# A four-layer decoder trunk: where the transposes of the next sub-layer's tokens stand, and which engine fills four zero tiles

## The chip, the cores and the metric

The kernel runs on one core of a Trainium2 chip. The metric is the device time of one execution in microseconds (us), taken as the median of several runs. The engines are TensorE (PE in the profile, with its weight loads as PEld), VectorE (DVE), ScalarE (ACT), GpSimd (POOL) and SyncE (SP, which here only issues DMAs). Each engine takes its instructions strictly in the order in which the built program holds them.

## The reference

256 tokens of 1024 float32 numbers pass through eight sub-layers: stick-breaking attention, an MLP, a short gated convolution, an MLP, gated linear attention (GLA), an MLP, stick-breaking attention, an MLP. Each sub-layer is wrapped in two RMS norms, and every MLP is the same:

```
def squared_relu_mlp(xn, w_up, w_down):
    return jnp.square(jax.nn.relu(xn @ w_up)) @ w_down

for i in range(DEPTH):                       # DEPTH = 4
    xn = rms_norm(h, norm_gains[i, 0])
    m = ...                                  # mixer i % 3 on xn
    h = h + rms_norm(m, norm_gains[i, 1])
    f = squared_relu_mlp(rms_norm(h, norm_gains[i, 2]), ffn_w_up[i], ffn_w_down[i])
    h = h + rms_norm(f, norm_gains[i, 3])
```

## The kernel before

The 256 tokens are two tiles, t = 0 and t = 1, of 128 tokens each; the residual stream `h` stays in SBUF. Every float32 operand of a large product is split in two parts, hi (rounded) and lo (the rest), and a product is three matmuls: hi by hi, hi by lo, lo by hi. The weights stream in as units of 1024 columns (SP issues the DMA into a ring of 5 `raw` buffers, ACT makes `hi` at L202 and DVE makes `lo` at L203, in rings of 9, each unit in two halves); 6 units are asked for ahead of their use.

A sub-layer ends with a product whose result has tokens on partitions: `out_proj_steps` (L368) for the three mixers, `down` in `ffn` (L421) for the MLP. It does t = 0 first and then t = 1, and the last part of each tile is 8 k-steps of six matmuls of 512 columns (hi, lo, and hi again, two PSUM banks each). After the last k-step of a tile `finish` (L849) runs: `add_norm` (L240: the square sums on ACT at L237, the product with the gain on DVE at L250, the reciprocal root on POOL at L229 and L232, the new h on DVE at L253), then `pre_norm` (L264) for the next sub-layer (again a square sum on ACT, the gain at L271, the root on POOL, and the scaling of both halves of the row at L279 on DVE). Then `turned` (L282) puts eight 128x128 transposes on PE (L262), four into each of two `wk` tiles in PSUM, and `spread` (L288) writes them into the stationary operands `xth` (ACT, L222) and `xtl` (DVE, L223).

The next sub-layer begins with a product that needs all of `xth` and `xtl` of one token tile at a time: `x_proj_steps` (L323) in the mixers, `up_x` (L386) in the MLP, 8 k-steps of six matmuls for t = 0 and then 8 for t = 1. In `up_x` the result goes through ACT (relu, L398) and DVE (square, L400) and is itself transposed, 8 more instructions of L262.

The order on each engine is made by a scheduler: an instruction has a priority from its place in the text, `tc.high_priority(offset=...)` moves it ahead by an offset, and the scheduler fills each engine in the order of priority as it reckons operands to be ready. Before, the transposes of t = 0 have the offset 400 and those of t = 1 the offset -80 (`TP`, L855); `add_norm`, `pre_norm` and `spread` have 400 (`HP`). Stick-breaking attention also needs four tiles of 1024 columns filled with zeros (`qpad`), filled on POOL at L456 in both layers that use it.

In the names below `s` is a working tile, `acc` and `wk` are PSUM tiles, `cf` holds the identity matrix, `sm` the small results of a norm.

Of the kernel before, what the change touches and what calls it, by code (L numbers as in the profile page):

```python
# [9 lines left out]
F32 = mybir.dt.float32  # L10
F32R = mybir.dt.float32r
# [5 lines left out]
P = 128  # L17
# [3 lines left out]
SEQ = 256  # L21
# [40 lines left out]
def hybrid_kernel(ctx: ExitStack, tc: tile.TileContext, x, norm_gains, sb_w_qkv, sb_w_o,  # L62
                  conv_w_in, conv_w, conv_w_out, gla_w_in, gla_w_gate_up, gla_b_gate,
                  gla_head_norm, gla_w_o, ffn_w_up, ffn_w_down, const_f, const_i, out,
                  phases=None, LA=6, RAW=5, RING=9, SLOTS=20, HP=400, AP=200, EP=200, XP=-40, TP=(400, -80),
                  F1=5.9, F2=1.3, G0=2.0, G1=2.0, LAG=1, PS=2,
# [48 lines left out]

    # residual stream and constants
    h = []
# [17 lines left out]

    # ---- weights, in the order of their first use
    plan = []
    index = {}

    def add(key, w, k0, n, c0, b):  # L140
        """n k-tiles of b columns, in pieces of 1024 columns a partition."""
        a = UNIT // b
        for j in range(n // a):
            index[(key, j)] = len(plan)
            plan.append(((key, j), rows(w, k0 + j * a, a, c0, b), b))
# [73 lines left out]

    # ---- pieces  # L220
    def split(hi, lo, src):
# [18 lines left out]
    def add_norm(accs, l, i, t, dst=None):  # L240
        """h += norm(the columns in accs); stored in halves where dst is given."""
        g = gain(l, i)
        ag = scratch()
        ss = []
        c = 0
        for a in accs:
            cs = slice(c, c + a.shape[1])
            c += a.shape[1]
            ss.append(sumsq(a))
            nc.vector.tensor_tensor(out=ag[:, cs], in0=a, in1=g[:, cs], op=ALU.mult)  # L250
        r = rstd_of(ss[0], 1, *ss[1:])
        for n, cs in enumerate([slice(0, D)] if dst is None else [slice(0, 512), slice(512, D)]):
            nc.vector.scalar_tensor_tensor(out=h[t][:, cs], in0=ag[:, cs], scalar=r, in1=h[t][:, cs], op0=ALU.mult, op1=ALU.add)  # L253
            if dst is not None:
                (nc.sync, nc.scalar)[n].dma_start(out=dst[:, cs], in_=h[t][:, cs])
# [32 lines left out]
    def spread(ws, t):  # L288
        for half, w in enumerate(ws):
            wv = w.rearrange("p (a b) -> p a b", b=P)  # L290
            sl = (slice(None), slice(4 * half, 4 * half + 4), slice(t * P, (t + 1) * P))
            split(xth[sl], xtl[sl], wv)

    def banks(acc):
        return [acc[:, 0:512], acc[:, 512:1024]]

    def x_stat(acc, lh, ll, units, first, last):
        """acc[n] += x.T @ units; lh/ll(kt) stationary, units: list over kt of [(hi, lo) per n]."""
        for _ in x_stat_steps(acc, lh, ll, units, first, last):
            pass  # L300
# [17 lines left out]
    def wide(key, j):  # L318
        """a k-tile of 1024 columns as the moving side."""
        hi, lo = need(key, j)  # L320
        return [(hi[:, 0, n * 512:(n + 1) * 512], lo[:, 0, n * 512:(n + 1) * 512]) for n in range(2)]

    def x_proj_steps(acc, t, key):  # L323
        lh, ll = xs(t)
        for j in range(KT):
            yield from x_stat_steps(banks(acc), lh[j:], ll[j:], [wide(key, j)], j == 0, j == KT - 1)

# [6 lines left out]
    def w_stat_steps(o, key):  # L334
        """o [P, 2, 256] = (two 128-column blocks of the unit).T @ x.T"""
        for k in range(KT):
            hi, lo = need(key, k // 4)
            for j in range(2):
                cs = slice(j * P, (j + 1) * P)
                oj = o[:, j * SEQ:(j + 1) * SEQ]  # L340
                mm(oj, hi[:, k % 4, cs], xth[:, k, :], k == 0 and j == 0, False)
                mm(oj, hi[:, k % 4, cs], xtl[:, k, :], False, False)
                mm(oj, lo[:, k % 4, cs], xth[:, k, :], False, k == KT - 1)
            yield 0.65
# [5 lines left out]
    class Fill:  # L350
        """Steps of matmuls, emitted in between the steps of a chain."""

# [15 lines left out]
    def out_proj_steps(l, us, finish):  # L368
        for t in range(NT):
            acc = acc_tile()  # L370
            ts = slice(t * P, (t + 1) * P)
            for j in range(KT):
                yield from x_stat_steps(banks(acc), [us[j // 4][0][:, j % 4, ts]], [us[j // 4][1][:, j % 4, ts]],
                                        [wide((l, "o"), j)], j == 0, j == KT - 1)
            finish([acc], t)
# [3 lines left out]

    # ---- FFN  # L380
    def ffn(l, finish, final=False):
# [4 lines left out]
        def up_x():  # L386
# [3 lines left out]
            for t in range(NT):  # L390
                acc = acc_tile()
                lh, ll = xs(t)
                for k in range(4):
                    un = [need((l, "up", g, k)) for g in range(XG)]
                    ws = [[(hi[:, a, :], lo[:, a, :]) for hi, lo in un] for a in range(2)]
                    x_stat(banks(acc), lh[2 * k:], ll[2 * k:], ws, k == 0, k == 3)
                r = scratch()
# [23 lines left out]
        def down(g, ts_):  # L421
            for k in range(4):
                for t in ts_:
                    if accs[t] is None:
# [25 lines left out]

    # ---- stick-breaking attention
    def sb(l, finish):
        qpad = []
        for i in range(4):
            q = slot((P, 2, 2, SEQ), F32R)
            nc.gpsimd.memset(q.bitcast(F32), 0.0)  # L456
            qpad.append(q)
        vs = []
        if l == 0:
            # both token tiles are there from the start: they share each piece of the weights  # L460
            accs = [acc_tile() for _ in range(NT)]
            gens = [x_proj_steps(accs[t], t, (l, "v")) for t in range(NT)]
            for j in range(KT + LAG):
                for t in range(NT):
                    if 0 <= j - LAG * t < KT:
                        next(gens[t])
        for t in range(NT):
# [4 lines left out]
            else:  # L472
                nc.scalar.copy(out=v, in_=acc)
            vs.append(v)
        us = [u_pair(), u_pair()]

        def qk_steps(g, res):
            w = wk_tile()
            yield from w_stat_steps(w, (l, "q", g))
            # the queries of each head of a pair, padded with zeros in the other head's rows  # L480
            qs = []
# [86 lines left out]

    # ---- short gated convolution
    def conv(l, finish):  # L570
# [45 lines left out]

    # ---- gated linear attention
    def gla(l, finish):
# [25 lines left out]

        # the gates' logarithms, tokens on partitions
        w = wk_tile()
# [34 lines left out]
        def decays(t, pr):  # L681
            """exp of the summed log gates between each token and the middle of its block, two levels."""
            acc = acc_tile()
# [32 lines left out]
        def weigh(t, pr):  # L716
            """the decays times the keys (lower halves) and the queries (upper halves), in place."""
            ts = slice(t * P, (t + 1) * P)
# [101 lines left out]

    # ---- the trunk
    pre = {"ffn": 2}
# [23 lines left out]
    for n, (kind, l) in enumerate(phases):  # L846
        nxt = phases[n + 1] if n + 1 < len(phases) else None

        def finish(acc, t, kind=kind, l=l, nxt=nxt):  # L849
# [4 lines left out]
            if nxt:  # L854
                with tc.high_priority(offset=TP[t]):  # L855
                    ws = turned(xn, t)
                with tc.high_priority(offset=HP):
                    spread(ws, t)

# [31 lines left out]
```

## Time and profile before

| | |
|---|---|
| time, median of 3 runs | 1228.62 us (1225.62 to 1228.74) |
| profiled execution, first to last instruction (its span, the only time of its own that the profile gives) | 1226.1 us |
| PE matmuls busy | 1193.8 us, 97% of the span, 7260 instructions |
| DVE / ACT / POOL busy | 769.4 / 671.5 / 57.3 us |
| chain that ended last, by engine | PE 46%, DVE 1%, POOL 1%, ACT 1% |
| granted TensorE clock, mean | 0.996 |
| HBM | 213 MB read, 175 GB/s over the span |

PE is busy nearly all the time, so what can be read for a change of order is where PE is idle and what ended each idle stretch. In a timeline row the numbers are the start, the length, the engine, the line, the operation, output and inputs, how many instructions the row merges, and in brackets the idle time of that engine before it with what ended it. Matmuls are pipelined: a matmul's row is longer than the distance to the next one, so distances are taken between starts.

### The profile page before, as it was taken

The page shows a single profiled execution, that of the slowest core. Times are in us where ns is not written, and L with a number is a line of the kernel's source. Part 1 is how long each engine was busy: PE and PEld are TensorE (multiplying, and loading weights), DVE is VectorE, ACT ScalarE, POOL GpSimd, SP SyncE. Part 2 cuts the span into 40 slices and gives each one's busy share as a digit, 9 for nine tenths or more (in the row PEclk, how much of TensorE's full clock was granted, in tenths as well). Part 3 has the DMA queues.
Part 4 walks back from the last instruction along what each step waited for, and adds up shares of the span by engine and source line. Part 5 has one row for each costly group of instructions (what it writes and reads, how often), then busy time and mean ns, then how long its engine had stood idle before and what let it go on. Part 6 is the DMA issues. An engine that isn't in the chain of part 4 may idle for free.

```text
span 1226.1 us, 18808 instructions
## 1 busy us (share of the span) xinstructions
PE 1193.8 (97%) x7260; PEld 1052.0 (86%) x7260; DVE 769.4 (63%) x1199; ACT 671.5 (55%) x1192; POOL 57.3 (5%) x94
## 2 busy tenths in 40 slices
PE   5999999999999999999999999999999999999997
PEld 4988789988799789988789878999877987899986
DVE  6675775654777666555656677655556666765552
ACT  5677564543555465554563655645544876554551
POOL 2000100000100100000200120000011000000000
PEclk9999999999999999999999999999999999999999
DMA  7743467566476556666553345666646442666540
GB/s 246 261 135 106 138 192 223 187 190 205 138 223 191 164 182 221 189 189 214 166 195 127 114 143 189 210 194 188 204 154 202 122 149 95 203 205 191 189 154 35
DMA packets 123083, 215.28 MB, mean 176 GB/s; under 512 B 7729, under 2 KB 85681, under 8 KB 122994
## 3 DMA queue, kind: packets, MB, share of 16 engines
q1 hardware_dynamic: 122434, 213.28, 55.2%
q8 instruction: 57, 0.93, 0.3%
q10 hardware_dynamic: 432, 0.59, 0.1%
q0 software_dynamic: 128, 0.21, 0.1%
q14 instruction: 32, 0.26, 0.1%
HBM read 213.01 MB, written 1.05 MB: 175 GB/s over the span
## 4 chain that ended last, share of the span: by engine, by line
PE 46%; DVE 1%; issue 1%; POOL 1%; ACT 1%; DMA 0%; DVEq 0%; POOLq 0%
PE acc L112 26%; PE wk L112 18%; PE wk L262 1%; DVE lo L203 0%; POOL sm L229 0%; POOL sm L232 0%; DMA raw<-in_sb_w_qkv_dram 0%; DVE s L279 0%; ACT s L237 0%; POOL s L760 0%; ACT s L535 0%; ACT s L773 0%; ACT hi L202 0%; DVE s L759 0%; DVE s L775 0%
## 5 line engine op out<-in xcount | busy, mean ns | idle before, releaser
L203 DVE TENSOR_TENSOR lo<-raw,hi 128x512 fp32r<-128x512 f32 x768 | 501.0, 688 | 268.0 <-ACT hi L202 265.5
L202 ACT CAST hi<-raw 128x512 fp32r<-128x512 f32 x768 | 442.4, 618 | 346.9 <-PE wk L112 169.2
L112 PE MATMUL acc<-hi,s 128*128 128x512 f32 x1280 | 355.1, 391 | 0.0
L112 PE MATMUL wk<-xth,hi 128*128 128x256 f32 x1216 | 342.1, 281 | 0.4 <-DVE s L585 0.4
L112 PE MATMUL wk<-xtl,hi 128*128 128x256 f32 x1216 | 342.0, 281 | 0.0
L112 PE MATMUL wk<-xth,lo 128*128 128x256 f32 x1216 | 341.3, 281 | 0.0
L112 PEld LDWEIGHTS acc<-hi,s 128*128 128x128 f32 x1280 | 237.9, 188 | 49.2 <-ACT s L222 1.3
L112 PEld LDWEIGHTS wk<-xth,hi 128*128 128x128 f32 x1216 | 229.3, 189 | 2.6 <-issue 0.7
L112 PEld LDWEIGHTS wk<-xtl,hi 128*128 128x128 f32 x1216 | 229.1, 188 | 1.3 <-issue 0.2
L112 PEld LDWEIGHTS wk<-xth,lo 128*128 128x128 f32 x1216 | 229.5, 189 | 0.2 <-issue 0.2
L112 PE MATMUL acc<-lo,s 128*128 128x512 f32 x640 | 199.6, 390 | 0.0
L112 PEld LDWEIGHTS acc<-lo,s 128*128 128x128 f32 x640 | 120.0, 188 | 25.0
L112 PE MATMUL acc<-hi,xth 128*128 128x512 f32 x288 | 95.7, 409 | 1.1 <-ACT xth L222 1.1
L112 PE MATMUL acc<-hi,xtl 128*128 128x512 f32 x288 | 94.4, 406 | 0.0
L112 PE MATMUL acc<-lo,xth 128*128 128x512 f32 x288 | 93.6, 405 | 0.0
L112 PEld LDWEIGHTS acc<-hi,xth 128*128 128x128 f32 x288 | 54.7, 192 | 13.9 <-ACT xth L222 1.7
L229 POOL TENSOR_SCALAR sm<-sm 128x1 f32<-128x1 f32 (+1 forms) x32 | 17.1, 536 | 1058.1 <-ACT s L237 1050.8
L112 PEld LDWEIGHTS acc<-hi,xtl 128*128 128x128 f32 x288 | 54.8, 191 | 13.6
L112 PEld LDWEIGHTS acc<-lo,xth 128*128 128x128 f32 x288 | 54.7, 191 | 13.2 <-issue 0.2
L250 DVE TENSOR_TENSOR s<-acc,s 128x1024 f32<-128x1024 f32 (+1 forms) x17 | 19.7, 1160 | 65.0 <-ACT s L237 65.0
L262 PE MATMUL wk<-cf,s 128*128 128x128 f32 x224 | 38.3, 288 | 22.5 <-DVE s L279 11.5
L262 PEld LDWEIGHTS wk<-cf,s 128*128 128x128 f32 x224 | 26.9, 146 | 31.5 <-issue 15.5
(101 smaller groups left out, 776.5 us busy)
## 6 DMA issues: line engine op xcount, KB each, us to landing
raw<-in_ffn_w_up_dram SPq DMA_DIRECT2D x128, 512.0 KB, 3.8
raw<-in_ffn_w_down_dram SPq DMA_DIRECT2D x128, 512.0 KB, 3.6
raw<-in_sb_w_qkv_dram SPq DMA_DIRECT2D x48, 512.0 KB, 4.8
raw<-in_conv_w_in_dram SPq DMA_DIRECT2D x24, 512.0 KB, 3.8
raw<-in_gla_w_in_dram SPq DMA_DIRECT2D x24, 512.0 KB, 4.1
s<-in_norm_gains_dram SPq DMA_DIRECT2D x16, 512.0 KB, 5.1
raw<-in_sb_w_o_dram SPq DMA_DIRECT2D x16, 512.0 KB, 3.6
raw<-in_conv_w_out_dram SPq DMA_DIRECT2D x8, 512.0 KB, 3.5
```

What stands on the lines that cost most here:

```text
L112: nc.tensor.matmul(out=o, lhsT=l, rhs=r, start=start, stop=stop, skip_group_check=True)
L202: nc.scalar.copy(out=hi[:, cs], in_=raw[:, cs])
L203: nc.vector.tensor_tensor(out=lo[:, cs], in0=raw[:, cs], in1=hi[:, cs].bitcast(F32), op=ALU.subtract)
L229: nc.gpsimd.tensor_scalar(out=v, in0=ss, scalar1=EPS, scalar2=None, op0=ALU.add)
L250: nc.vector.tensor_tensor(out=ag[:, cs], in0=a, in1=g[:, cs], op=ALU.mult)
L262: nc.tensor.transpose(out=dst[:, j * P:(j + 1) * P], in_=src[:, j * P:(j + 1) * P], identity=ident)
```

## The change

Priorities no longer place the transposes. `finish` only puts the scaled tile in a list, `pending`, and the products call `turn_pending` at a fixed k-step: the products that end a sub-layer after their sixth k-step of t = 1 (`TURN[0]`; this turns the tokens of t = 0), and the products that begin one after their seventh k-step of t = 0 (`TURN[1]`; this turns the tokens of t = 1). The writes into `xth` and `xtl` keep their priority. In the second stick-breaking layer the four zero tiles are filled by DVE, after the values of t = 0 are copied, in place of POOL at the start of the layer; the first such layer is as before. The diff, without comment lines and with the loops that it goes through:

```
-                  ... XP=-40, TP=(400, -80),
+                  ... XP=-40, TURN=(6, 7),
...
+    pending = []
+
+    def turn_pending():
+        while pending:
+            xn, t = pending.pop()
+            ws = turned(xn, t)
+            with tc.high_priority(offset=HP):
+                spread(ws, t)
...
     def x_proj_steps(acc, t, key):
         for j in range(KT):
+            if j == TURN[1]:
+                turn_pending()
...
     def out_proj_steps(l, us, finish):
             for j in range(KT):
+                if j == TURN[0]:
+                    turn_pending()
...
         def up_x():
-                    x_stat(banks(acc), lh[2 * k:], ll[2 * k:], ws, k == 0, k == 3)
+                    for j, _ in enumerate(x_stat_steps(banks(acc), lh[2 * k:], ll[2 * k:], ws, k == 0, k == 3)):
+                        if 2 * k + j + 1 == TURN[1]:
+                            turn_pending()
...
         def down(g, ts_):
             for k in range(4):
+                if 4 * (g - 6) + k == TURN[0]:
+                    turn_pending()
...
     def sb(l, finish):
+        def padded(eng):
+            for i in range(4):
+                q = slot((P, 2, 2, SEQ), F32R)
+                eng.memset(q.bitcast(F32), 0.0)
+                qpad.append(q)
         qpad = []
-        for i in range(4):
-            q = slot((P, 2, 2, SEQ), F32R)
-            nc.gpsimd.memset(q.bitcast(F32), 0.0)
-            qpad.append(q)
+        if l == 0:
+            padded(nc.gpsimd)
...
             vs.append(v)
+            if l and t == 0:
+                padded(nc.vector)
...
         def finish(acc, t, kind=kind, l=l, nxt=nxt):
             if nxt:
-                with tc.high_priority(offset=TP[t]):
-                    ws = turned(xn, t)
-                with tc.high_priority(offset=HP):
-                    spread(ws, t)
+                pending.append((xn, t))
```

First place: PE at the end of the first attention layer, in the product of t = 1 (a k-step's matmuls are named by their weight, here `hi_1104` for the sixth and `hi_1184` for the seventh). Before:

```order
L112 MATMUL acc_1361<-hi_1050,s_378 128x512 x2
L112 MATMUL acc_1361<-hi_1104,s_377 128x512
L262 MATMUL wk_1347<-cf_84,s_1336 128x128 x4
L262 MATMUL wk_1348<-cf_84,s_1336 128x128 x4
L112 MATMUL acc_1361<-hi_1104,s_377 128x512
L112 MATMUL acc_1361<-lo_1105,s_377 128x512 x2
```

and now:

```order
L112 MATMUL acc_1347<-hi_1050,s_378 128x512 x2
L112 MATMUL acc_1347<-hi_1104,s_377 128x512 x2
L112 MATMUL acc_1347<-lo_1105,s_377 128x512 x2
L112 MATMUL acc_1347<-hi_1104,s_378 128x512 x2
L262 MATMUL wk_1384<-cf_84,s_1336 128x128 x4
L262 MATMUL wk_1385<-cf_84,s_1336 128x128 x4
L112 MATMUL acc_1347<-hi_1184,s_377 128x512 x2
```

The eight transposes of t = 0 stand five matmuls later, behind 36 of the 48 in place of 31; all seven sub-layer ends have this shift. On ACT at the same place (`hi` are weight casts, `xth` the write that the transposes release), before:

```order
L202 CAST hi_1296<-raw_1294 128x512 x2
L202 CAST hi_1310<-raw_1308 128x512
L222 CAST xth_93<-wk_1347 128x4x128
L222 CAST xth_93<-wk_1348 128x4x128
L202 CAST hi_1310<-raw_1308 128x512
```

and now:

```order
L202 CAST hi_1310<-raw_1308 128x512 x2
L202 CAST hi_1438<-raw_1436 128x512
L222 CAST xth_93<-wk_1384 128x4x128
L222 CAST xth_93<-wk_1385 128x4x128
L202 CAST hi_1438<-raw_1436 128x512
```

Two weight casts that stood behind the writes into `xth` stand ahead of them; DVE has the same with two `lo` ahead of `xtl`.

Second place: PE in the MLP that follows, in the product of t = 0 (`acc_1449`, now `acc_1435`). Before:

```order
L112 MATMUL acc_1449<-lo_1453,xth_93 128x512
L112 MATMUL acc_1449<-lo_1461,xth_93 128x512
L262 MATMUL wk_1431<-cf_84,s_1420 128x128
L112 MATMUL acc_1449<-hi_1452,xtl_94 128x512
L262 MATMUL wk_1431<-cf_84,s_1420 128x128
L112 MATMUL acc_1449<-hi_1460,xtl_94 128x512
L262 MATMUL wk_1431<-cf_84,s_1420 128x128
```

and now:

```order
L112 MATMUL acc_1435<-lo_1447,xth_93 128x512
L112 MATMUL acc_1435<-hi_1438,xtl_94 128x512
L112 MATMUL acc_1435<-hi_1446,xtl_94 128x512
L262 MATMUL wk_1542<-cf_84,s_1420 128x128 x4
L262 MATMUL wk_1543<-cf_84,s_1420 128x128 x4
L112 MATMUL acc_1435<-hi_1438,xth_93 128x512
```

The transposes of t = 1 stand together behind 42 matmuls; before they stood one by one between matmuls, the first behind 40. The first transposes behind matmuls stood at 42 in the convolution, 38 in GLA and 41 in the second attention layer, and stand at 42 in all of them now. The MLP's own transposes, of its squared result, stand behind 11 matmuls of t = 1 in place of 12.

Third place: the second attention layer. POOL before (`sm` are the steps of the norms of t = 1):

```order
L232 TENSOR_TENSOR sm_8949<-sm_8950,mhalf_91 128x1
L456 MEMSET s_8979 128x1024
L229 TENSOR_SCALAR sm_8960<-sm_8955 128x1
L456 MEMSET s_8981 128x1024
L232 TENSOR_TENSOR sm_8959<-sm_8960,mhalf_91 128x1
L456 MEMSET s_8983 128x1024
L456 MEMSET s_8985 128x1024
```

and DVE there now:

```order
L271 TENSOR_TENSOR s_8954<-h_81,s_8869 128x1024
L203 TENSOR_TENSOR lo_8997<-raw_8994,hi_8996 128x512
L279 TENSOR_SCALAR s_8954<-s_8954,sm_8959 128x512 x2
L203 TENSOR_TENSOR lo_8997<-raw_8994,hi_8996 128x512
L223 TENSOR_TENSOR xtl_94<-wk_9064,xth_93 128x4x128
L223 TENSOR_TENSOR xtl_94<-wk_9065,xth_93 128x4x128
L493 COPY s_9092<-acc_8965 128x1024
L474 MEMSET s_9094 128x1024
L203 TENSOR_TENSOR lo_9011<-raw_9008,hi_9010 128x512 x2
L474 MEMSET s_9096 128x1024
```

POOL has no fills left there; DVE has them behind the copy of the values (two more follow eight `lo` later), and one `lo` where it had two between L271 and L279.

## Rows read from the trace of the kernel before

**Rows 1.** The page's busy time of the engines: us, share of the span, instructions.

```profile
PE 1193.8 (97%) x7260; PEld 1052.0 (86%) x7260; DVE 769.4 (63%) x1199; ACT 671.5 (55%) x1192; POOL 57.3 (5%) x94
```

**Rows 2.** The view of waits, PE alone: who waited for whom, us in total, times, the longest.

```profile
PE wk L262 <- DVE s L279: 11.5, 10, 2.8
```

**Rows 3.** The timeline of PE: the start of the program, the end of the first attention layer, and the end of the third MLP.

```profile
18.24 1.60 PE L262 MATMUL wk<-cf,s 128*128 128x128 f32 x8 [2.77 <-DVE s L279]
...
131.50 0.84 PE L112 MATMUL acc<-hi,s 128*128 128x512 f32 x3
133.17 1.09 PE L262 MATMUL wk<-cf,s 128*128 128x128 f32 x8 [0.83 <-DVE s L279]
...
907.59 0.84 PE L112 MATMUL acc<-hi,s 128*128 128x512 f32 x3
909.35 1.06 PE L262 MATMUL wk<-cf,s 128*128 128x128 f32 x8 [0.92 <-DVE s L279]
```

**Rows 4.** The timeline at the end of the first attention layer: the issue of the weights on SP (the row merges six) and the weight casts of ACT around the next square sum.

```profile
130.15 10.37 SPq L197 DMA_DIRECT2D raw<-in_ffn_w_up_dram  x6
...
134.82 1.77 ACT L202 CAST hi<-raw 128x512 fp32r<-128x512 f32 x3
137.83 1.14 ACT L202 CAST hi<-raw 128x512 fp32r<-128x512 f32 x2 [1.24 <-DMA raw<-in_ffn_w_up_dram]
138.88 1.02 ACT L237 ACTIVATE s<-acc 128x1024 f32<-128x1024 f32 x1
```

**Rows 5.** The timeline of t = 1: the scaling on DVE and PE's transposes, in the first MLP (with ACT's last step before), the convolution, the second MLP and GLA.

```profile
144.06 0.18 ACT L237 ACTIVATION_READ_ACCUMULATOR s<-h 128x1 f32 x1
146.16 0.88 DVE L279 TENSOR_SCALAR s<-s,sm 128x512 f32<-128x512 f32 x2 [0.77 <-POOL sm L232]
147.33 0.27 PE L262 MATMUL wk<-cf,s 128*128 128x128 f32 x1
150.09 0.40 PE L112 MATMUL acc<-hi,xth 128*128 128x512 f32 x1
...
329.44 0.88 DVE L279 TENSOR_SCALAR s<-s,sm 128x512 f32<-128x512 f32 x2 [0.77 <-POOL s L600]
331.15 0.49 PE L262 MATMUL wk<-cf,s 128*128 128x128 f32 x3
...
425.34 0.88 DVE L279 TENSOR_SCALAR s<-s,sm 128x512 f32<-128x512 f32 x2 [0.77 <-POOL sm L232]
426.61 0.27 PE L262 MATMUL wk<-cf,s 128*128 128x128 f32 x1
...
609.03 0.63 PE L112 MATMUL acc<-hi,xth 128*128 128x512 f32 x2
609.48 0.88 DVE L279 TENSOR_SCALAR s<-s,sm 128x512 f32<-128x512 f32 x2 [0.46 <-POOL sm L232]
613.36 0.63 PE L112 MATMUL acc<-hi,xth 128*128 128x512 f32 x2
```

**Rows 6.** The timeline of the second attention layer, t = 1.

```profile
914.15 0.63 PE L112 MATMUL acc<-hi,xth 128*128 128x512 f32 x2
920.14 0.19 ACT L237 ACTIVATION_READ_ACCUMULATOR s<-h 128x1 f32 x1
920.41 1.75 POOL L229 TENSOR_SCALAR sm<-sm 128x1 f32<-128x1 f32 x1 [2.57 <-DMA raw<-in_sb_w_qkv_dram]
920.79 1.29 DVE L203 TENSOR_TENSOR lo<-raw,hi 128x512 fp32r<-128x512 f32 x2
922.22 0.95 POOL L456 MEMSET s<- 128x1024 f32 x1
923.14 0.57 POOL L232 TENSOR_TENSOR sm<-sm,mhalf 128x1 f32<-128x1 f32 x1
923.48 0.40 PE L112 MATMUL acc<-hi,xtl 128*128 128x512 f32 x1
923.65 1.85 POOL L456 MEMSET s<- 128x1024 f32 x2
923.74 2.42 DVE L279 TENSOR_SCALAR s<-s,sm 128x512 f32<-128x512 f32 x2 [1.66 <-POOL sm L232]
925.92 0.30 PE L262 MATMUL wk<-cf,s 128*128 128x128 f32 x1 [2.05 <-DVE s L279]
930.05 0.40 PE L112 MATMUL acc<-hi,xth 128*128 128x512 f32 x1
```

**Rows 7.** Stretches: start:end and length; busy time (instructions) of PE, PEld, DVE, ACT and POOL; the granted TensorE clock; the share and rate of DMA.

```profile
131.50:134.10 2.60, 1.77 (x13) 1.31 (x11) 1.83 (x5) 1.92 (x5) 1.01 (x2) 1.00 0.56 182
152.90:154.00 1.10, 1.10 (x10) 1.05 (x10) 0.48 (x1) 1.10 (x3) 0.00 (x0) 1.00 0.00 0
926.56:929.97 3.41, 3.41 (x13) 2.76 (x11) 1.38 (x2) 1.17 (x2) 0.00 (x0) 0.50 0.00 0
930.05:948.30 18.25, 18.25 (x109) 16.06 (x108) 12.87 (x19) 11.79 (x21) 0.00 (x0) 1.00 0.71 227
```

**Rows 8.** Zero or constant fills: the view by line for DVE's only fill of some size (ns: shortest, median, longest) and for POOL's (busy us, mean ns).

```profile
L130 DVE MEMSET mones<- x1: 165/165/165, 0.8 to 0.8; 128x128 f32 x1
...
L456 POOL MEMSET s<- 128x1024 f32 x8 | 7.5, 957 | 0.1
```

**Rows 9.** The timeline of the first MLP between the end of its first product and its own transposes.

```profile
150.54 1.03 ACT L398 ACTIVATE s<-acc 128x1024 f32<-128x1024 f32 x1
151.60 1.23 DVE L400 TENSOR_TENSOR s<-s 128x1024 f32<-128x1024 f32 x1 [0.24 <-ACT s L398]
```

More of the change, by code (lines that the diff above doesn't have):

```diff
@@ L64, in hybrid_kernel @@
                   gla_head_norm, gla_w_o, ffn_w_up, ffn_w_down, const_f, const_i, out,
-                  phases=None, LA=6, RAW=5, RING=9, SLOTS=20, HP=400, AP=200, EP=200, XP=-40, TP=(400, -80),
+                  phases=None, LA=6, RAW=5, RING=9, SLOTS=20, HP=400, AP=200, EP=200, XP=-40, TURN=(6, 7),
                   F1=5.9, F2=1.3, G0=2.0, G1=2.0, LAG=1, PS=2,
```

## The prediction

> **What bounds the kernel now.** I read the page's busy times first: PE works 97% of the span [rows 1], and no other engine comes near, so only an idle stretch of PE can be won. Then the view of waits of PE alone: the largest sum there is transposes waiting for the scaled rows of the next tokens (L279 on DVE), 11.5 us in ten waits [rows 2]. Then the timeline, to see where the ten are. One of 2.77 us is at the start of the program [rows 3], which the change leaves alone; one of 2.05 us is in the second attention layer [rows 6]; one is in GLA, t = 1, and the other seven, about 6.3 us, are the seven ends of sub-layers, t = 0, of which two are shown [rows 3].
>
> Brackets understate what PE loses, because the row of the last matmul outlasts the distance to the next one. From 914.15 to 923.48 lie 40 matmuls [rows 6], 0.2333 us from start to start. At the end of the first attention layer the three matmuls from 131.50 would let the next instruction start at 132.20; it starts at 133.17, 0.97 us late, where the bracket says 0.83 [rows 3]. At the end of the third MLP it is 908.29 against 909.35, 1.06 us late for 0.92 [rows 3]. So each bracket is short by 0.14.
>
> **The change part by part.**
>
> *t = 0, seven ends.* The loss is 6.3 + 7 x 0.14 = 7.3 us. The transposes now stand five matmuls later, 5 x 0.2333 = 1.17 us, and that is more than the 0.97 to 1.06 by which the scaled rows came late, so PE finds them ready, with 0.1 to 0.2 us to spare. The chain up to L279 (ACT, DVE, POOL) has the same order as before. I take 7.2 won; bounds 4 (each place keeps 0.4) and 7.3.
>
> What pays for it: after the transposes, 12 matmuls (2.8 us) now stand before the next sub-layer reads `xth`, where 17 did, and ACT has two weight casts ahead of the write. The eight transposes take about 0.93 us with the step to the next matmul (133.17, a row of 1.09 [rows 3]), so `xth` is wanted 3.7 us after their start. Without the casts ACT would start 0.7 us in; with both it needs up to 1.2 us (three take 1.77 [rows 4]) and then 0.6 per half. Written by 2.4 us, it is 1.3 early. The price is nothing while those casts find their weights. The unit was asked for at 130.15, and its casts ran without a pause by 134.82 to 136.6 [rows 4]. That is the weak point; a rival below prices it.
>
> *t = 1, four MLPs and the convolution.* Here PE did not wait. It now arrives earlier by what t = 0 won, but two matmuls later in order in the MLPs (+0.47) and none in the convolution. Does L279 move earlier too? I think not: the square sum of t = 1 at 138.88 follows two casts that waited for a weight transfer until 137.83 [rows 4], and that transfer does not move. So the first MLP's transposes go from 147.33 to 147.33 - 0.97 + 0.47 = 146.83, against a first half of the scaled row ready about 0.5 us after 146.16 plus 0.1, at 146.75 [rows 5]. The second MLP: 426.61 - 1.06 + 0.47 = 426.02 against 425.93. The convolution: 331.15 - 1.06 = 330.09 against 330.03 [rows 5]. All pass, with less than 0.1 us to spare. Standing together instead of between matmuls costs nothing: 147.33 to 150.09 holds eight transposes and eight matmuls [rows 5], 2.76 - 1.87 = 0.89 us for the transposes, against 0.93.
>
> *t = 1 in GLA.* PE would come to the transposes at 609.03 + 0.47 + four more matmuls 0.93 - 1.06 = 609.37, and the scaled row is there at about 610.06 [rows 5]: a wait of 0.7 us. Then 0.93 and six matmuls of 1.40 put the product of t = 1 at 612.39, where it was 613.36 [rows 5], 0.97 earlier; of the 1.06 brought in, 0.1 is lost.
>
> *t = 1 in the second attention layer.* POOL's root waited in a queue with zero fills: L229 1.75 us, a fill of 0.95, L232 0.57, and then L279 took 2.42 us beside two more fills, where it takes 0.88 elsewhere [rows 5, 6]. Without the fills, and with one `lo` ahead of L279 in place of two, I use the delay of the first MLP, from 144.25 to 146.16, 1.91 us [rows 5]. From 920.33 that gives L279 at 922.24 and the first half at PE by 922.8. PE arrives at 914.15 - 1.06 + 42 x 0.2333 = 922.89. Then 0.93 + 1.40, and the product of t = 1 starts at 925.22 in place of 930.05 [rows 6], 4.83 earlier, 3.77 beyond what t = 0 gave. [...] Bounds: 2 (a second wait of 1.8) and 4.
>
> The row of L229 ends as the two `lo` beside it end, with no fill running [rows 6]. [...]
>
> *Zero fills on DVE.* DVE's only fill has 128 columns and took 0.165 us [rows 8]. The cost of 1024 columns is bounded by that (no less) and eight times that, 1.3; POOL's 0.957 lies between. I take 1.0 each, 4.0 for four. From 930.05 to 948.30 DVE works 12.87 of 18.25 us [rows 7], so 5.4 are free, and PE uses weights six units after they are asked for. I take 0.1 lost; bounds 0 and 1.
>
> *The MLP's own transposes.* They stand behind 11 matmuls of t = 1 in place of 12, 2.57 us after its start. The square needs 1.03 + 1.23 from a start of 0.45 (150.54 against 150.09), and was ready at 152.83 [rows 5, 9], 2.74 after. ACT can start a little earlier now. So between 0 and 0.27 is lost, 0.1 taken, four times: 0.4.
>
> **Sum.** 7.2 + 3.8 - 0.1 - 0.1 - 0.4 = 10.4 us. The profiled execution's span is 1226.1 us, which gives 1215.7; the median of the timed runs is 2.5 above that execution, and the prediction in medians is 1218.2, so 1218.
>
> **The rivals.**
>
> *The wait passes to t = 1.* For it: the scaled rows of t = 1 do not move and the margins above are under 0.1 us. Against: nothing ahead of L279 in those chains has become longer. If they come 0.5 us late at six places, 3 us go back and the time is 1221; if all that t = 0 won is given back, only 3.1 stay and it is 1225.5.
>
> *The second attention layer gains nothing*, because DVE, with four fills, is late with the split queries. 6.6 stay: 1222. Against: the 5.4 us free.
>
> *The clock falls at transposes that stand together.* In the second attention layer the eight transposes and seven matmuls from 925.92 to 930.05 took 4.13 us at half clock for most of it, against 0.89 + 1.63: 1.6 more [rows 6, 7]. At seven places that is 11.3, and the time is 1229.5, no change. Against: the clock was granted at 1.00 around the eight together at 133.17 and around the MLP's own at 152.98 [rows 7]. [...]
>
> *Slower: ACT stands at a weight cast ahead of `xth`.* `xth` is wanted 3.7 us after the transposes' start at 133.4, so the moved cast must begin by about 135.8 (0.6 for it, 0.6 for the half). It ran by 135.4 before. If the transfer landed later, each us beyond costs PE one us at each of seven ends: 1.5 beyond eats the gain, and 2.5 beyond gives 17.5 - 10.4 = 7 slower, 1236. Against: the transfer is issued by an event that does not move.
>
> **How the numbers follow.** Forecast 0.66, its own range 1215 to 1221 (the runs before spread over 3 us); the wait passing on 0.15, of which 0.04 within 0.3%; the attention layer 0.08; the clock 0.05; slower 0.06. About 0.3%, 3.7 us, is what a measurement of this kernel can tell from no change. Faster: 0.66 + 0.11 + 0.08 = 0.85; same 0.04 + 0.05 = 0.09; slower 0.06. The range 1214 to 1224 leaves out the last two rivals and the far end of the first. Below 1214 nothing in the rows points.
>
> **What would show it.** Right: the waits of PE for L279 fall from 11.5 to about 3.5 us (the start and GLA); PE's rows before L262 at the seven ends carry no bracket; L279 in the second attention layer takes 0.88 us and no half clock follows; the span is near 1216. Wrong: brackets at t = 1 of 0.5 us and more; the first `xth` of a sub-layer waited for by PE; the clock at 0.50 near L262; DVE's fills with PE waiting behind them.

## The result, and the profile after

The changed kernel takes 1218.11 us (median of 4 runs, 1217.59 to 1219.75), the kernel before in the same rounds 1228.68; the ratio is 0.9919 [0.9907, 0.9931], about 10 us faster. The forecast was 1218.0, the range 1214 to 1224. The span of the profiled execution fell from 1226.1 to 1216.1 us. One of the ten timed runs of e1 (below) took 3039 us and is left out of its median.

The page's busy times and the waits of PE (us in total, times, the longest), which answer to [rows 1, 2]:

```profile
PE 1190.9 (98%) x7260; PEld 1051.6 (86%) x7260; DVE 770.4 (63%) x1203; ACT 670.2 (55%) x1192; POOL 52.4 (4%) x90
```

```profile
PE wk L262 <- DVE s L277: 9.6, 1, 9.6
PE wk L262 <- DVE s L279: 3.2, 2, 2.7
```

The sum for L279 fell from 11.5 us in ten waits to 3.2 in two: the start of the program, 2.66, and GLA, 0.52. (L277 is the first wait of the program, for the first tokens.) The four instructions that DVE has more and POOL has less are the zero fills.

The timeline of PE at the end of the first attention layer and of the third MLP, which answers to [rows 3]:

```profile
134.01 0.62 PE L112 MATMUL acc<-hi,s 128*128 128x512 f32 x2
134.47 1.04 PE L262 MATMUL wk<-cf,s 128*128 128x128 f32 x8
...
138.11 0.63 PE L112 MATMUL acc<-hi,xth 128*128 128x512 f32 x2
...
905.48 1.03 PE L262 MATMUL wk<-cf,s 128*128 128x128 f32 x8
```

There is no bracket ahead of L262, and the distance from 134.01 to 134.47, 0.46 us, is that of the pairs of matmuls ahead of it (0.45 from 132.20 to 132.65 and from 133.56 to 134.01). By the view of waits none of the other five ends has one either. The next reader of `xth` starts at 138.11, 3.64 us after the transposes (3.7 forecast).

The issue on SP and the timeline of ACT at the same place, which answer to [rows 4]:

```profile
131.30 0.38 SPq L197 DMA_DIRECT2D raw<-in_ffn_w_up_dram  x1
```

```profile
132.16 3.43 ACT L202 CAST hi<-raw 128x512 fp32r<-128x512 f32 x6
135.50 1.07 ACT L222 CAST xth<-wk 128x512 fp32r<-128x512 f32 x2
139.13 1.14 ACT L202 CAST hi<-raw 128x512 fp32r<-128x512 f32 x2 [2.05 <-DMA raw<-in_ffn_w_up_dram]
```

Six weight casts run without a pause up to `xth`, whose two halves are written from 135.50 to 136.57, 1.5 us before they are wanted. The cast that waits for its transfer comes 139.13 - 131.30 = 7.83 us after the issue; before it was 137.83 - 130.15 = 7.68 [rows 4]. Counted from its issue the transfer comes no sooner, and the issue is 1.15 us later, by about as much as the whole program is behind its start (below).

The timeline of t = 1 in the first MLP (DVE, then PE), in GLA, and in the second attention layer, which answers to [rows 5, 6], and one stretch of that layer as in [rows 7]:

```profile
147.14 0.88 DVE L279 TENSOR_SCALAR s<-s,sm 128x512 f32<-128x512 f32 x2 [0.46 <-POOL sm L232]
147.91 1.04 PE L262 MATMUL wk<-cf,s 128*128 128x128 f32 x8
...
605.80 0.96 POOL L652 MEMSET s<- 128x1024 f32 x1
...
607.96 1.06 PE L262 MATMUL wk<-cf,s 128*128 128x128 f32 x8 [0.52 <-DVE s L279]
...
916.50 1.15 POOL L229 TENSOR_SCALAR sm<-sm 128x1 f32<-128x1 f32 x1 [3.38 <-ACT s L237]
...
918.33 0.88 DVE L279 TENSOR_SCALAR s<-s,sm 128x512 f32<-128x512 f32 x2 [0.77 <-POOL sm L232]
918.96 1.06 PE L262 MATMUL wk<-cf,s 128*128 128x128 f32 x8
...
922.85 0.91 DVE L474 MEMSET s<- 128x1024 f32 x1 [0.16 <-issue]
```

```profile
918.00:922.00 4.00, 4.00 (x24) 3.24 (x23) 3.24 (x6) 1.07 (x2) 0.30 (x1) 1.00 0.48 142
```

By its brackets PE stands nowhere at t = 1 but in GLA. In the second attention layer L279 takes 0.88 us in place of 2.42 and the clock stays granted at 1.00. In GLA a POOL fill still stands ahead of L232, which follows it at 606.72.

From PE's arrival behind the 31st matmul of the first sub-layer's end (132.20 before; after, 134.47 less five matmuls of 0.23, so 133.3) to the end of the span it was 1093.9 us and is 1082.8: 11.1 won. The start of the program was 1.1 us later in the execution profiled after.

### The profile page after: what moved, and what is told of

It is laid out like the page before. It is cut to its first block, busy times and chain, and to the rows that moved or that the text cites. A ratio compares the mean times of both kernels' runs of the same rounds, so it can differ in the third digit from the quotient of the medians.

```text
span 1216.1 us, 18811 instructions
## 1 busy us (share of the span) xinstructions
PE 1190.9 (98%) x7260; PEld 1051.6 (86%) x7260; DVE 770.4 (63%) x1203; ACT 670.2 (55%) x1192; POOL 52.4 (4%) x90
## 4 chain that ended last, share of the span: by engine, by line
PE 93%; issue 3%; ACT 1%; DVE 1%; DMA 1%; POOL 1%; SPq 0%; DVEq 0%; POOLq 0%; ACTq 0%
PE acc L112 54%; PE wk L112 37%; PE wk L262 2%; DMA raw<-in_sb_w_qkv_dram 1%; DMA raw<-in_gla_w_in_dram 0%; ACT hi L202 0%; POOL sm L232 0%; ACT s L559 0%; ACT s L237 0%; POOL s L784 0%; DVE lo L203 0%; DVE s L279 0%; POOL sm L229 0%; DVE h L253 0%; ACT s L797 0%
## 5 line engine op out<-in xcount | busy, mean ns | idle before, releaser
L250 DVE TENSOR_TENSOR s<-acc,s 128x1024 f32<-128x1024 f32 (+1 forms) x17 | 19.7, 1161 | 65.3 <-ACT s L237 65.0
L229 POOL TENSOR_SCALAR sm<-sm 128x1 f32<-128x1 f32 (+1 forms) x32 | 15.2, 476 | 1053.8 <-ACT s L237 1049.1
L112 PE MATMUL acc<-s,s 128*128 128x256 f32 (+3 forms) x316 | 51.5, 336 | 2.3 <-ACT s L559 1.8
L237 ACT ACTIVATE s<-acc 128x1024 f32<-128x1024 f32 (+1 forms) x17 | 16.6, 974 | 63.3 <-PE acc L112 63.3
```

The source lines that it names most:

```text
L112: nc.tensor.matmul(out=o, lhsT=l, rhs=r, start=start, stop=stop, skip_group_check=True)
L229: nc.gpsimd.tensor_scalar(out=v, in0=ss, scalar1=EPS, scalar2=None, op0=ALU.add)
L237: nc.scalar.activation(out=scratch()[:, 0:src.shape[1]], in_=src, func=AF.Square, scale=1.0 / 32.0, accum_out=ss)
```

## Experiments

Medians are given with the ratio to the kernel before in the same rounds. "From the first end" means from that arrival behind 31 matmuls to the end of the span, which leaves the start of the program out.

**e1: the fills alone.** The kernel before, with the second attention layer's fills moved behind the values of t = 0 and put on DVE.

```
-            nc.gpsimd.memset(q.bitcast(F32), 0.0)
...
+        if l == 0:
+            padded(nc.gpsimd)
...
+            if l and t == 0:
+                padded(nc.vector)
```

> The kernel before, with the second attention layer's four zero fills on DVE and nothing else. By my terms the 2.05 us wait of PE there and the stretch at half clock go, and the seven waits at t = 0 stay with brackets of 0.83 to 0.94 us: 3.8 us faster than before, 1224.9. If the fills have no part in that wait (it is made by the place of the transposes), the wait stays at 2 us and the time is 1228.7.

1224.95 us (median of nine runs), ratio 0.9967 [0.9957, 0.9976]. The seven brackets stand as before (0.92 at the end of the third MLP, as there) and the second attention layer has none. From the transposes at the end of the third MLP to those at the end of this layer (last of each eight) it takes 120.1 us where it took 124.1: 4.0 won.

**e2: the places alone.** The changed kernel with the fills back on POOL, ahead of the layer.

```
-        if l == 0:
-            padded(nc.gpsimd)
+        padded(nc.gpsimd)
...
-            if l and t == 0:
-                padded(nc.vector)
```

> The changed kernel, with the second attention layer's zero fills back on POOL. By my terms the seven waits at t = 0 are gone, but PE comes to the transposes of t = 1 in the second attention layer 0.8 us earlier, so that wait grows from 2.05 to 2.8 us or more with the half clock behind it: 6.5 us faster than before, 1222.2, so that the two parts add up to the whole. If the place alone were what matters, the wait there would be gone and the time 1218.

1221.41 us, ratio 0.9946 [0.9926, 0.9965]. The seven ends have no bracket. In the second attention layer (POOL, DVE and PE):

```profile
917.89 1.84 POOL L474 MEMSET s<- 128x1024 f32 x2
...
917.98 2.42 DVE L279 TENSOR_SCALAR s<-s,sm 128x512 f32<-128x512 f32 x2 [0.46 <-POOL sm L232]
...
920.16 1.06 PE L262 MATMUL wk<-cf,s 128*128 128x128 f32 x8 [1.75 <-DVE s L279]
```

The wait was expected to grow to 2.8 and did not even reach the 2.05 of [rows 6], and the clock stayed granted at 1.00. L229 was shorter this time, 0.55 us. The two parts, 3.9 and 7.5 us in medians against the kernel before of their rounds (1228.86), add up to the 10.6 of the whole within their intervals. The profiled executions do not add up: from the first end e1's is 4.9 us faster than that of before and e2's, the fastest of its five runs, 9.6, where the changed kernel's is 11.1. What the fills on POOL cost differs between executions; the account below comes back to it.

**e3: t = 0 one k-step earlier**, behind the 31 matmuls of the kernel before, with all else as changed.

```
- TURN=(6, 7)
+ TURN=(5, 7)
```

> The changed kernel with the tokens of t = 0 turned after the fifth k-step; the scheduler puts them behind 31 matmuls, where they stood before. By my terms the seven brackets of 0.83 to 0.94 us come back and nothing else: 7.2 us slower than the changed kernel, 1225.3. If the gain came from the transposes of t = 1 standing together and from the fills, this is as fast as the changed kernel, 1218.

1223.69 us, ratio 0.9964 [0.995, 0.9977]. All seven brackets are back, 0.83 to 0.93 us, the first of them:

```profile
132.99 1.09 PE L262 MATMUL wk<-cf,s 128*128 128x128 f32 x8 [0.83 <-DVE s L279]
```

From the first end it takes 1089.6 us against 1082.8: 6.8 slower, the size of the first term; in medians it is 5.6. So this term is won by the five matmuls alone. e3 differs from e1 in the place of the transposes of t = 1 and of the MLP's own: from the first end 1089.6 against 1089.1, so that these places by themselves win nothing that the runs show.

**e4: t = 0 one k-step later** (`TURN=(7, 7)`), so that 6 matmuls in place of 12 cover the write of `xth`.

> The changed kernel with the tokens of t = 0 turned after the seventh k-step, behind 42 matmuls, so that six matmuls instead of twelve cover the writes into xth. Transposes and six matmuls take 2.3 us; ACT writes the first half of xth 1.6 us after the transposes' start in the changed kernel. By my terms there is no wait, or one of up to 0.3 us at each end: 1218 to 1220. By the rival in which ACT stands at weight casts ahead of xth, the next sub-layer's first matmul waits 0.5 us or more at seven ends: 1221.5 or more.

1217.95 us, ratio 0.9915 [0.9896, 0.9934]. No wait at any end. ACT, then PE:

```profile
135.25 1.07 ACT L222 CAST xth<-wk 128x512 fp32r<-128x512 f32 x2 [0.41 <-PE wk L262]
...
136.88 0.63 PE L112 MATMUL acc<-hi,xth 128*128 128x512 f32 x2
```

Here ACT has done its weight casts and waits for PE. `xth` is whole at 136.3, 0.56 us before it is wanted.

**e9: t = 0 after the last matmul**, no cover at all.

```
- TURN=(6, 7)
+ TURN=(8, 7)
...
+            turn_pending()
             finish([acc], t)
```

The call stands behind the last k-step of each tile, in `out_proj_steps` and in `ffn`; behind that of t = 1 it turns the tokens of t = 0.

> The changed kernel, with the tokens of t = 0 turned behind the last matmul of the old sub-layer, so that no matmul stands between the transposes and the first reader of xth (12 do in the changed kernel). It prices the rival of the prediction that was to make the kernel slower (xth late). Theory: with twelve matmuls between them xth is ready some 1.5 to 2 us before it is wanted, and without any PE must wait for the write of the first half: this write ends about 1.2 us after the transposes' start (0.63 to its start and 0.6 for the half) and the transposes take 0.93, so PE waits about 0.3 us at each of seven ends, and perhaps as much again for xtl: 2 to 5 us in all, median 1220 to 1223. Rival (ACT and DVE stand at weight casts there, or the clock falls at the wait): over 1 us at each end, median above 1226. Other rival (PE does not notice): 1218.

1235.51 us, ratio 1.007 [1.0046, 1.0095]: slower than the kernel before. The theory falls, and so does "PE does not notice"; the size is that of the first rival, but neither cause that it named accounts for it: the granted clock fell at one of the seven ends only (from 1.00 to 0.50, at the end of the convolution), and there are no weight casts in the way. The first end, where the transposes start at 138.17, on ACT, PE and DVE:

```profile
138.43 1.02 ACT L237 ACTIVATE s<-acc 128x1024 f32<-128x1024 f32 x1 [1.50 <-PE acc L112]
139.44 1.06 ACT L222 CAST xth<-wk 128x512 fp32r<-128x512 f32 x2
```

```profile
140.07 0.73 PE L112 MATMUL acc<-hi,xth 128*128 128x512 f32 x2 [0.87 <-ACT xth L222]
142.25 0.74 PE L112 MATMUL acc<-hi,xtl 128*128 128x512 f32 x2 [0.97 <-DVE xtl L223]
```

```profile
140.38 1.22 DVE L250 TENSOR_TENSOR s<-acc,s 128x1024 f32<-128x1024 f32 x1
141.51 1.28 DVE L223 TENSOR_TENSOR xtl<-wk,xth 128x512 fp32r<-128x512 f32 x2
```

Not a weight cast stands ahead of `xth`, but the square sum of t = 1 (L237): the same last matmul that now precedes the transposes sets it free, and ACT takes it first. On DVE the product with the gain (L250) does the same to `xtl`. Each end loses about 2.5 us (17.4 us in medians, over seven). The price of the rival that was to make the kernel slower is real, but it begins with less than 6 matmuls of cover, not with 12, and its cause is another.

**e5: t = 1 one k-step earlier** (`TURN=(6, 6)`).

> The changed kernel, with the tokens of t = 1 turned after the sixth k-step in place of the seventh (six matmuls, 1.4 us, earlier at all seven places). Theory (the scaled rows of t = 1 hang on casts that wait for their weights and do not move with PE; the margin at the four MLPs and the convolution is about 0.1 to 0.3 us): PE waits for L279 about 1.1 to 1.3 us at each of these five places and at GLA about 0.9 more than the 0.52 it has; the second attention layer, which has most to spare, waits up to 1. PE waits for L279 in all rise from 3.2 to about 10 us, span about 1223 to 1224, median about 1225 to 1226. Rival (the chain of t = 1 has slack, or moves with PE): no more than 0.3 us at a place, and the median stays at 1218 to 1220.

1227.31 us, ratio 1.0 [0.999, 1.001]: the whole win is gone. PE waits at all seven places of t = 1, 1.03 to 1.34 us. The first MLP, on ACT, DVE and PE:

```profile
139.39 1.14 ACT L202 CAST hi<-raw 128x512 fp32r<-128x512 f32 x2 [1.92 <-DMA raw<-in_ffn_w_up_dram]
```

```profile
147.40 0.88 DVE L279 TENSOR_SCALAR s<-s,sm 128x512 f32<-128x512 f32 x2 [0.46 <-POOL sm L232]
```

```profile
148.03 1.06 PE L262 MATMUL wk<-cf,s 128*128 128x128 f32 x8 [1.03 <-DVE s L279]
```

L279 starts 147.40 - 139.39 = 8.01 us after the cast that waits for a transfer, and in the changed kernel 147.14 - 139.13 = 8.01 too. PE came 1.4 us earlier and the chain did not follow. This run moves neither the old sub-layer's product nor the transfers, on which the chain hangs, so it measures the margin and does not tell why the chain stands still. By the brackets the six matmuls less the waits leave a margin in the changed kernel of 1.40 - 1.34 = 0.06 to 1.40 - 1.03 = 0.37 us, outside GLA. But each bracket is short by about 0.14, as the prediction worked out, so the margin is nothing to 0.2 us. The starts in the changed kernel agree: from the new product's first matmul to the transposes the 42 matmuls take 9.80 us, and it is 9.80 at the four MLPs, 330.22 - 320.39 = 9.83 in the convolution and 918.96 - 909.10 = 9.86 in the second attention layer. I had put that layer among those with the most to spare; it has none.

**e6: the first attention layer's fills on DVE too.**

```
-        if l == 0:
-            padded(nc.gpsimd)
...
-            if l and t == 0:
+            if t == 0:
                 padded(nc.vector)
```

> The changed kernel, with the first attention layer's zero fills on DVE as well (in the changed kernel these four stay on POOL). At the start of the program the trace of the changed kernel shows the same picture as the second attention layer before the change: a POOL fill between L229 and L232, L279 at 2.42 us beside two more fills, PE waiting 2.66 us, half clock around it. Theory: POOL's fills are the cause there too, so L279 falls to 0.88 us, the wait to 0.3 or less, and the time from the first transposes to the end falls by 2 to 3 us: median 1215 to 1216. Rival (the start is bounded by transfers or by the clock's coming up, the wait passes to something else): median 1217.5 to 1218.5, with a new wait of PE in the first 25 us.

1214.19 us, ratio 0.9893 [0.9878, 0.9908]: below the changed kernel by 3.9 us in medians, by 3.2 in the ratios. The start of the program in the changed kernel (POOL, DVE, PE) and then in this one:

```profile
15.48 0.95 POOL L474 MEMSET s<- 128x1024 f32 x1
...
16.92 1.85 POOL L474 MEMSET s<- 128x1024 f32 x2
...
17.01 2.42 DVE L279 TENSOR_SCALAR s<-s,sm 128x512 f32<-128x512 f32 x2 [1.67 <-POOL sm L232]
...
19.19 1.09 PE L262 MATMUL wk<-cf,s 128*128 128x128 f32 x8 [2.66 <-DVE s L279]
```

```profile
13.47 0.99 POOL L229 TENSOR_SCALAR sm<-sm 128x1 f32<-128x1 f32 x1 [7.39 <-ACT s L237]
...
15.15 0.88 DVE L279 TENSOR_SCALAR s<-s,sm 128x512 f32<-128x512 f32 x2 [0.77 <-POOL sm L232]
15.79 1.23 PE L262 MATMUL wk<-cf,s 128*128 128x128 f32 x8 [0.23 <-DVE s L279]
```

The wait that the prediction set aside as part of the start has the same cause as that of the second attention layer. The gain is at or above the top of the 2 to 3 us expected. From the first transposes of the program to the first end (last of each eight) the profiled executions take 124.1 us and 120.8: 2.4 of these 3.3 are the wait, and the rest I put down to the clock, which was granted at 0.52 in the mean from 20 to 23 us in the changed kernel and at 1.00 from 17 to 30 us in this one. What is above 3.3 lies in the start before the first transposes, which begin between 8.3 and 9.7 us in the profiled executions here.

**e7: GLA's two fills on DVE as well.**

```
-            nc.gpsimd.memset(a.bitcast(F32), 0.0)
+            nc.vector.memset(a.bitcast(F32), 0.0)
```

> As the one before, and GLA's two zero fills (the first a rows of the gate, 1024 columns each) on DVE instead of POOL as well. Theory: GLA's transposes of t = 1 wait 0.5 us for L279, whose sum was made on POOL beside such a fill; if the fill is the cause the wait falls to under 0.2 and the median is 0.3 to 0.5 us below the kernel without this edit. Rival (the wait comes from PE being early, by ACT's casts): the wait of about 0.4 to 0.5 stays, the median is the same within 0.3 us.

1213.96 us, ratio 0.9894 [0.9878, 0.9911]. GLA's wait is gone (0.41 in e6), with POOL's L232 right behind L229; in medians 0.2 less, which the runs cannot tell from none.

**e10: all fills on DVE and `TURN=(7, 7)`**, and **e11: the changed kernel again**.

> The changed kernel with t = 0 turned after the seventh k-step too, and all zero fills (first attention layer and GLA) on DVE. The two edits act at different places, so the parts should add: the fills gave about 4 us (1214.0 to 1214.2 against 1218.1), the seventh in place of the sixth nothing by itself. Theory: median 1213.5 to 1214.5, as with the fills alone, PE without a wait for L279 but 0.2 to 0.5 at the start. Rival (what PE gains at the start lets it come to the casts ahead of xth at t = 0 too early): waits of PE for xth at the seven ends, 0.2 us and more each, median 1215.5 to 1217.

> The changed kernel once more, unaltered, on the chip and in the rounds of the kernel above, as its reference: median 1217.5 to 1218.5. Its profile also tells how far the start of the program and GLA's wait vary from one execution to the next: the wait of the first t = 1 transposes 2.6 to 2.8 us, GLA's 0.3 to 0.5.

e10: 1213.32 us, ratio 0.9878 [0.9862, 0.9894], the fastest here, with a wait for L279 of 0.55 at the start. e11: 1217.3, ratio 0.9916 [0.9903, 0.9929], with waits of 2.66 and 0.28. There is no wait for `xth` at the ends of e10. The fills carry its gain; the interval overlaps that of e7.

**e12: the fills at the new place, but on POOL.** This tells the place from the engine.

```
-                padded(nc.vector)
+                padded(nc.gpsimd)
```

> The changed kernel, with the second attention layer's four zero fills at their new place in the program (behind the values of t = 0) but on POOL, as before, so that they stand behind L229 and L232 of t = 1 in POOL's queue. It tells the place from the engine. Theory (the fills cost by standing between L229 and L232 and by running beside L279): at the new place on POOL they do neither as long as they start after L232, so PE's wait in the second attention layer stays at zero or under 0.4 us and the median is 1217 to 1219. Rival (a fill on POOL holds up DVE wherever it stands, so the split queries come late, or the scheduler of POOL lets them run beside L279 all the same): PE waits 0.7 us or more at or behind the transposes of the second attention layer, and the median is 1219 to 1221.

1222.95 us, ratio 0.9958 [0.9943, 0.9973]; from the first end 3.6 us slower than the changed kernel. The theory falls and the rival holds, at more than the rival's price (1219 to 1221). POOL, DVE and PE in the second attention layer, and the stretch behind it:

```profile
917.99 0.57 POOL L232 TENSOR_TENSOR sm<-sm,mhalf 128x1 f32<-128x1 f32 x1
918.49 3.63 POOL L474 MEMSET s<- 128x1024 f32 x4
...
918.59 4.21 DVE L279 TENSOR_SCALAR s<-s,sm 128x512 f32<-128x512 f32 x2 [0.77 <-POOL sm L232]
...
922.56 1.06 PE L262 MATMUL wk<-cf,s 128*128 128x128 f32 x8 [3.21 <-DVE s L279]
```

```profile
922.56:926.00 3.44, 3.44 (x20) 3.02 (x21) 3.00 (x5) 1.08 (x2) 0.00 (x0) 1.00 0.39 121
```

The four fills start as soon as L232 is done, 0.10 us ahead of L279, and L279's first half takes 3.82 us and ends only behind the last of them (922.41 against 922.12). Out of the chain's way in POOL's queue, they cost 3.5 us from the end of the third MLP to that of this layer, where they cost 2.1 in e2, in its way (122.6 and 121.2 us against 119.1 in the changed kernel). The timed runs of e12 and e2 overlap, so that this order rests on the two profiled executions.

## Why the prediction was right, and where it was off

*t = 0, seven ends.* Forecast 7.2 won. All brackets are gone, and undoing this alone costs 6.8 in the profiled execution and 5.6 in medians (e3). The slack of 0.1 to 0.2 us by which the scaled rows were to be early was enough at all seven.

*What pays for it.* `xth` was to be written 1.3 us early; it was 1.5. The weak point, weight casts ahead of it, holds with half the cover (e4). The price that I gave the slower rival, 1236, is met by e9, but by work that I had not thought of: the square sum and the gain product of t = 1. That the two numbers agree is chance.

*t = 1, MLPs and convolution.* "The chain does not move" holds. Its place is read from PE's first matmul of the new product, in the first MLP here before and after:

```profile
138.00 0.63 PE L112 MATMUL acc<-hi,xth 128*128 128x512 f32 x2
...
138.11 0.63 PE L112 MATMUL acc<-hi,xth 128*128 128x512 f32 x2
```

L279 starts 146.16 - 138.00 = 8.16 us behind it before [rows 5] and 147.14 - 138.11 = 9.03 after. At the five places it is 7.8 to 8.2 before, 8.9 to 9.2 after and 7.8 to 8.5 in e3, which takes the win of t = 0 back: PE came about 1 us earlier and the chain stayed. At each of the five ACT waits for a weight transfer ahead of the chain, 0.86 to 1.25 us before and 1.83 to 2.28 after; in the first MLP that wait ends 7.68 us behind the issue before and 7.83 after. That the margins were thin (under 0.1 forecast, nothing to 0.2 measured) made this the real danger: one k-step less gives the whole win back (e5). The rival "the wait passes to t = 1" was the right one to fear, and, since the margins there are below the 0.47 us of the two matmuls by which the MLPs' transposes were moved back, PE would by this reckoning have waited without those; no run tried it.

*GLA.* A wait of 0.7 was forecast; 0.52, 0.28 and, without its fill, none were measured.

*Second attention layer.* Forecast 3.8; e1 alone gave 4.0. L279 was to take 0.88 and did. The size was right against the profiled execution of before, and in part by luck: 1.6 of it was the half clock of that execution, and in e2's, where the clock stayed at 1.00, the fills cost 2.1 in the same stretch (3.3 in medians, 1221.41 against 1218.11). The reason was half the story: I counted the fill in POOL's queue and the slow L279 together. In e12 POOL's queue delays nothing, and the slow L279 alone, beside four fills in place of two, costs 3.6. L229's row, which ended 0.08 us behind the two `lo` beside it [rows 6], stayed slow without the fills: in the changed kernel it took 1.15 us beside L271 and one `lo`, both with two inputs in SBUF, and ended 0.09 behind the `lo`; at 912.24, beside L250, which has one input in PSUM, it took 0.22. What makes the difference no run tells.

*Zero fills on DVE.* 1.0 us each forecast, 0.91 measured with 0.16 ahead of it; PE does not wait behind them.

*The MLP's own transposes.* I charged 0.4 for four. In the timeline there is no bracket ahead of any of them. They start 0.30 to 0.36 us behind the matmul before them, where it was 0.30 to 0.32 before the change: under 0.1 lost in all four. This term was mis-sized.

*The sum.* 10.4 was forecast, 11.1 came from the first end on. The start of the profiled execution, 1.1 us later than that of before, and a median that lies 2.0 above the span in place of 2.5, brought the time back to the forecast: a part of the closeness is luck.

*The clock rival.* The clock was granted at 1.00 around the fourteen groups of eight at the seven ends, t = 0 and t = 1.

## What to carry to other kernels

Where PE waits a fixed time for a chain, place the consumer by counting matmuls, and count both margins: how late the producer is, and how much cover is left for the next one. Here the window at t = 0 is two k-steps wide (sixth or seventh), at t = 1 one step earlier loses everything, and a step later was not tried.

Before a small wait is called part of the start, look whether it has the same rows as a wait elsewhere: POOL fills in and beside a norm cost PE 2 to 4 us at two places and half a us at a third, and the change mended one of the three.

## What the runs showed of the hardware that I had not expected

*POOL's fills held up DVE's scaling, fill after fill.* L279's half row takes 0.48 us in the median; beside two fills its two halves take 2.42 (e2), beside four 4.21 (e12), about the length of the fills (1.84 and 3.63) plus half a row. The length is in the first half, 2.03 us in e2 and 3.82 in e12. The fills are not slowed: those of e12 take 0.945 to 0.964 us each, and in the changed kernel the one in GLA that ends before L279 starts takes 0.96. The fills start 0.09 us ahead of L279 in e2 and 0.10 in e12, and DVE did not get in between four fills in a row. A fill on DVE did not do this to POOL: in e7 L232 keeps its 0.57 us beside one.

```profile
602.97 0.91 DVE L650 MEMSET s<- 128x1024 f32 x1 [0.16 <-DVE s L271]
602.97 0.57 POOL L232 TENSOR_TENSOR sm<-sm,mhalf 128x1 f32<-128x1 f32 x1
```

*The length of a wait did not tell whether the clock fell.* Behind 2.05 us the grant fell to 0.50 [rows 6, 7]. Behind 1.75 (e2) and 3.21 (e12) in the same place it stayed at 1.00. In e9 it fell behind waits of 0.80 and 1.03 at the end of the convolution, and not behind 0.87 and 0.97 at the first end:

```profile
424.00:428.00 4.00, 4.00 (x11) 3.19 (x12) 4.00 (x5) 2.29 (x4) 1.01 (x1) 0.58 0.55 171
...
142.00:146.00 4.00, 3.75 (x16) 3.07 (x17) 4.00 (x6) 2.29 (x4) 0.75 (x1) 1.00 0.59 181
```

What decides it these runs do not show. So the 1.6 us of half clock in the second attention layer belong to that execution; in how many others they occur stays open.
